# Hybrid decoder layer on one Trainium2 core: keys and values of the memory branch as one product of a transposed, unnormalised mem

## The chip, the cores and the metric

One core of a Trainium2 chip runs the whole layer as one program. The metric is the device time of an execution in microseconds (us). TensorE (PE in the views, its weight loads PEld) multiplies; VectorE (DVE), ScalarE (ACT) and GpSimd (POOL) do the rest; the queue of SyncE (SP) issues nearly all DMAs.

## The reference, cut to what matters

`d` = 1024, `s` = 512 rows of `x`, `m` = 256 rows of `mem`, four cross heads of 64.

```python
h = rms_norm(x, g_mix)                       # x * rsqrt(mean(x*x, row) + eps) * g
proj = h @ w_in                              # q, k, v, index q/k/w, conv, qc, gates
...
mem_kv = (rms_norm(mem, g_mem) @ w_mem_kv).reshape(b, m, 2, N_CROSS_HEADS, HEAD_DIM)
y_mem = memory_attention(qc, mem_kv[:, :, 0], mem_kv[:, :, 1]) @ w_mem_out
...
x = x + merged @ w_o                         # then norm, gated conv MLP, final norm
```

## The kernel before

Every product is made of three in fp32r: each operand is split into a high part `hi` (a copy on ACT to fp32r) and a low part `lo` (on DVE, source minus `hi`), and `mm3` (L144 to L147) adds hi·hi, hi·lo and lo·hi in one PSUM bank. Weights go through `load` (a DMA on SP's queue into tile `raw`) and `split` (L154 to L156) into `whi`/`wlo`; each of these three tags has three buffers, so a fourth load waits until an earlier one is split.

The program's order is a list of priorities. A planner that simulates the engines puts the instructions of each engine in a fixed order, in which they then run; the DMAs marked `first` stay in program order on SP's queue.

The first stage works off the memory tokens. `norm_rows` squares a block of 128 rows on ACT with a running sum, makes the inverse root on POOL, and multiplies rows, root and gain in one DVE instruction into `xn`. `turn_rows` transposes `xn` in eight 128x128 pieces on PE (L173) into two PSUM banks, and splits these into `mT` (for mem) or `h` (for x). The gain `g_mem` is loaded as `gm`, broadcast to 128 partitions (512 KB). Then 48 matmuls of 256 columns give the values (tokens in rows, `mT` is the stationary operand), split into `VM`; 48 more give the keys already transposed (`w_k` is stationary), copied to `kf`, and with `halves` and `twice` to `KM`. Both are read only in the cross attention, far later.

The second stage makes value and index columns of `w_in` (`w_n`, four tiles of 256 rows and 424 columns) for four blocks of `x`: 24 matmuls of 424 columns for each block. In the source the norm of block b+1 stands behind the products of block b. Its index columns are rotated (`rn`) and transposed (L306, L309). From there on `project` multiplies further columns of `w_in` with all of `h`, 24 matmuls of 512 columns each.

Of the kernel before, what the change touches and what calls it, by code (L numbers as in the profile page):

```python
# [10 lines left out]
F32 = mybir.dt.float32  # L11
F32R = mybir.dt.float32r
# [78 lines left out]


@with_exitstack
def layer(ctx, tc, x, mem, g_mix, g_mem, g_ffn, g_final, w_in, w_n, w_k, w_v, w_cm, w_att, w_o, w_up, w_down,
          params, rope, rope_n, out):
    nc = tc.nc

# [8 lines left out]
    def bank(tag="mm"):  # L106
        return ps.tile([P, 512], F32, tag=tag, name="ps_" + tag, bufs=banks[tag])
# [13 lines left out]

    def load(src, sp=wp, bufs=3):
        raw = sp.tile(list(src.shape), F32, tag="raw", name="raw", bufs=bufs)
        return raw, nc.sync.dma_start(raw, src)

    def split_load(raw, sp=wp, bufs=3):
        shape = list(raw.shape)
        hi = sp.tile(shape, F32R, tag="whi", name="whi", bufs=bufs)
        lo = sp.tile(shape, F32R, tag="wlo", name="wlo", bufs=bufs)
        split(hi, lo, raw)  # L130
        return hi, lo

    def wsplit(src, sp=wp):
        raw, _ = load(src)
        with tc.high_priority(offset=400):
            return split_load(raw, sp)

# [6 lines left out]
    def mm3(o, sh, sl, mh, ml, first, last):  # L144
        nc.tensor.matmul(o, sh, mh, start=first, stop=False)  # L145
        nc.tensor.matmul(o, sh, ml, start=False, stop=False)  # L146
        nc.tensor.matmul(o, sl, mh, start=False, stop=last)  # L147

    def gemm(o, w, act, kc=KD, k0=0):
        for k in range(kc):  # L150
            mm3(o, w[0][:, k0 + k, :], w[1][:, k0 + k, :], act[0][:, k, :], act[1][:, k, :],
                k == 0, k == kc - 1)

    def split(hi, lo, src):  # L154
        nc.scalar.activation(hi, src, AF.Copy)  # L155
        nc.vector.tensor_sub(lo, src, hi.bitcast(F32))  # L156

    def norm_rows(src, g, tmp):

        xn = tmp.tile([P, D], F32, tag="xn", name="xn", bufs=2)  # L160
        st = tmp.tile([P, 2], F32, tag="st", name="st", bufs=2)
        nc.scalar.activation(xn, src, AF.Square, accum_out=st[:, 0:1])
        nc.gpsimd.tensor_scalar(st[:, 0:1], st[:, 0:1], 1.0 / D, EPS, op0=ALU.mult, op1=ALU.add)
        nc.gpsimd.tensor_tensor(out=st[:, 1:2], in0=st[:, 0:1], in1=mhalf, op=ALU.pow)
        nc.vector.scalar_tensor_tensor(xn, src, st[:, 1:2], g, op0=ALU.mult, op1=ALU.mult)
# [23 lines left out]
    def bcast(g, n):  # L189
        return bass.AP(tensor=g.tensor, offset=g.offset, ap=[[0, P], [1, n]])  # L190
# [7 lines left out]
    oat = (op.tile([P, 3, S], F32R, name="oath"), op.tile([P, 3, S], F32R, name="oatl"))  # L198
    ocv = (op.tile([P, 3, S], F32R, name="ocvh"), op.tile([P, 3, S], F32R, name="ocvl"))
    ome = (op.tile([P, 2, S], F32R, name="omeh"), op.tile([P, 2, S], F32R, name="omel"))  # L200
# [3 lines left out]
    g0 = g0p.tile([P, KD, S], F32, name="g0")  # L204


    cs = ExitStack()
# [12 lines left out]

    es = ExitStack()
    ea = es.enter_context(pool("ea", side="right"))
    gm = ea.tile([P, D], F32, name="gm")
    gx = ea.tile([P, D], F32, name="gx")
    ropeN = ea.tile([P, 2, NB, 4], F32, name="ropeN")
    nc.scalar.dma_start(ropeN, rope_n)


    def first(dma):
        tc.keep_in_program_order(dma)  # L230

    def first_rows(src, b, slot):
        t = ea.tile([P, D], F32, tag=f"in{slot}", name="rows")
        first(nc.sync.dma_start(t, src[b * P:(b + 1) * P, :]))
        return t

    def first_load(src, *where):
        raw, dma = load(src, *where)
        first(dma)
        return raw  # L240
# [8 lines left out]
    mT = (ea.tile([P, KD, M], F32R, name="mTh"), ea.tile([P, KD, M], F32R, name="mTl"))  # L249
    norm_T(memn[0], gm, mT, 0, ea)  # L250
    wv[0] = split_load(wv[0])
    norm_T(memn[1], gm, mT, 1, ea)
    wk.append(first_load(w_k[1]))
    wn3 = first_load(w_n[3], ea, 1)
    wv[1] = split_load(wv[1])
    wn = [first_load(w_n[0])]
    xin.append(first_rows(x, 1, 0))
    wk[0] = split_load(wk[0])
    wn.append(first_load(w_n[1]))
    for b in range(MB):  # L260
        bs = slice(b * P, (b + 1) * P)
        pv = bank()
        for k in range(KD):
            w = wv[k // 4]
            mm3(pv[:, :CW], mT[0][:, k, bs], mT[1][:, k, bs], w[0][:, k % 4], w[1][:, k % 4], k == 0, k == KD - 1)
        split(VM[:, b, :, 0:HD], VM[:, b, :, HD:], pv[:, :CW].rearrange("p (h d) -> p h d", d=HD))
    norm_T(xin[0], gx, h, 0, ea)
    wk[1] = split_load(wk[1])
    wn.append(first_load(w_n[2]))
    xin += [first_rows(x, 2, 1), first_rows(x, 3, 2)]  # L270
    wn = [split_load(wn3, ea, 1)] + [split_load(w) for w in wn]
    kf = []
    for t in range(2):
        pb = bank()
        gemm(pb[:, :M], wk[t], mT)
        kf.append(ea.tile([P, M], F32, tag="kf", name="kf", bufs=2))
        nc.scalar.activation(kf[t], pb[:, :M], AF.Copy)
# [35 lines left out]

    def twice(K, r, j, hd, lo):
        a, q = slice(64 * j, 64 * j + 64), slice(64 - 64 * j, 128 - 64 * j)
# [495 lines left out]
```

## Time and profile before

| | us |
|---|---|
| runs | 1946.31, 762.21, 762.58 |
| median | 762.58 |
| profiled execution, its own time | 763.54 |
| its span, first to last instruction | 761.8 |
| TensorE busy in the span | 743.9 (98%) |
| VectorE busy | 465.9 (61%) |
| ScalarE busy | 339.1 (45%) |

The span lacks what lies around the first and the last instruction, 1.74 us of the profiled execution's time. Busy time is summed over the whole span and says nothing about a single stage.

### The profile page before, as it was taken

Reading aid. Unit: us, or ns where it says so; the run is one execution under the profiler, and the core shown is the slowest. Engines: PE = TensorE matmul, PEld = TensorE weight load, DVE = VectorE, ACT = ScalarE, POOL = GpSimd, SP = SyncE. Lnnn points to the kernel's source line nnn. Section 1 sums busy time; section 2 is a strip of 40 time slices with the busy share of each in tenths; the row PEclk is TensorE's granted clock in tenths of the full one; section 3 lists DMA queues with packets and bytes.
Section 4 is the critical chain, followed back from the end, with each engine's and each line's share of the span. In section 5 each row is a group of like instructions: output and inputs, shape, how many; then the busy total and the mean of one; then the engine's idle time right before and its main releaser. Section 6 shows DMA issues by size and latency. Waiting matters only on the chain.

```text
span 761.8 us, 9285 instructions
## 1 busy us (share of the span) xinstructions
PE 743.9 (98%) x3518; PEld 624.3 (82%) x3518; DVE 465.9 (61%) x793; ACT 339.1 (45%) x562; POOL 21.2 (3%) x49
## 2 busy tenths in 40 slices
PE   5999999999999999999999999999999999999996
PEld 4988888888888888888889888888888888888884
DVE  5744999999677765366465666566656664222225
ACT  5748545667455653234335343434343433121214
POOL 2100002000000000000010000000000000000001
PEclk9999999999999999999999999999999999999998
DMA  8623423532222223443502323232323232323202
GB/s 315 223 89 100 141 84 111 165 97 73 73 90 61 68 74 107 155 140 112 184 28 84 105 89 104 91 105 88 106 88 108 87 105 66 125 92 98 96 28 111
DMA packets 25181, 81.28 MB, mean 107 GB/s; under 512 B 3280, under 2 KB 4432, under 8 KB 25136
## 3 DMA queue, kind: packets, MB, share of 16 engines
q1 hardware_dynamic: 24848, 80.41, 32.0%
q8 instruction: 27, 0.44, 0.2%
q10 hardware_dynamic: 288, 0.28, 0.1%
q14 instruction: 18, 0.15, 0.1%
HBM read 75.24 MB, written 2.10 MB: 102 GB/s over the span
## 4 chain that ended last, share of the span: by engine, by line
PE 95%; DVE 2%; DMA 1%; ACT 1%; issue 1%; SPq 0%; POOL 0%; POOLq 0%; DVEq 0%
PE ps_mm L147 19%; PE ps_mm L145 19%; PE ps_mm L146 19%; PE ps_at L145 9%; PE ps_at L146 9%; PE ps_at L147 9%; PE ps_at L569 1%; PE ps_o L600 1%; PE ps_at L586 1%; PE ps_o L145 1%; PE ps_o L147 1%; PE ps_o L146 1%; PE ps_at L173 1%; DMA gm<-g_mem 1%; PE ps_at L380 1%
## 5 line engine op out<-in xcount | busy, mean ns | idle before, releaser
L156 DVE TENSOR_TENSOR wlo<-raw,whi 128x1024 fp32r<-128x1024 f32 (+3 forms) x133 | 157.2, 1185 | 198.3 <-ACT whi L155 198.3
L155 ACT ACTIVATE whi<-raw 128x1024 fp32r<-128x1024 f32 (+3 forms) x133 | 136.8, 1030 | 195.1 <-PE ps_o L147 82.1
L145 PE MATMUL ps_mm<-hhi,whi 128*128 128x512 f32 x312 | 122.5, 393 | 0.0
L146 PE MATMUL ps_mm<-hlo,whi 128*128 128x512 f32 x312 | 122.2, 392 | 0.0
L147 PE MATMUL ps_mm<-hhi,wlo 128*128 128x512 f32 x312 | 122.1, 392 | 0.0
L146 PE MATMUL ps_at<-h2l,whi 128*128 128x512 f32 (+1 forms) x216 | 78.9, 366 | 0.0
L147 PE MATMUL ps_at<-h2h,wlo 128*128 128x512 f32 (+1 forms) x216 | 78.9, 365 | 0.0
L145 PE MATMUL ps_at<-h2h,whi 128*128 128x512 f32 (+1 forms) x216 | 78.7, 366 | 0.0
L146 PEld LDWEIGHTS ps_mm<-hlo,whi 128*128 128x128 f32 x312 | 58.7, 188 | 11.8
L147 PEld LDWEIGHTS ps_mm<-hhi,wlo 128*128 128x128 f32 x312 | 58.6, 188 | 11.6
L145 PEld LDWEIGHTS ps_mm<-hhi,whi 128*128 128x128 f32 x312 | 58.6, 188 | 11.6
L145 PE MATMUL ps_mm<-h2h,whi 128*128 128x512 f32 x160 | 62.2, 389 | 0.0
L146 PE MATMUL ps_mm<-h2l,whi 128*128 128x512 f32 x160 | 62.2, 389 | 0.0
L147 PE MATMUL ps_mm<-h2h,wlo 128*128 128x512 f32 x160 | 62.2, 389 | 0.0
L147 PEld LDWEIGHTS ps_at<-h2h,wlo 128*128 128x128 f32 x216 | 40.7, 189 | 6.6
L146 PEld LDWEIGHTS ps_at<-h2l,whi 128*128 128x128 f32 x216 | 40.8, 189 | 6.4
L145 PEld LDWEIGHTS ps_at<-h2h,whi 128*128 128x128 f32 x216 | 40.6, 189 | 6.6
L145 PEld LDWEIGHTS ps_mm<-h2h,whi 128*128 128x128 f32 x160 | 30.0, 188 | 6.3
L147 PEld LDWEIGHTS ps_mm<-h2h,wlo 128*128 128x128 f32 x160 | 30.0, 188 | 6.3
L146 PEld LDWEIGHTS ps_mm<-h2l,whi 128*128 128x128 f32 x160 | 30.0, 188 | 6.1
L733 ACT ACTIVATE t<-t 128x512 f32<-128x512 f32 x22 | 13.9, 632 | 44.6 <-DVE t L415 44.5
L155 ACT ACTIVATE acth<-t 128x512 fp32r<-128x512 f32 x14 | 8.8, 632 | 40.4 <-DVE t L734 40.4
(246 smaller groups left out, 1316.0 us busy)
## 6 DMA issues: line engine op xcount, KB each, us to landing
raw<-w_up SPq DMA_DIRECT2D x44, 512.0 KB, 3.4
raw<-w_in SPq DMA_DIRECT2D x39, 512.0 KB, 3.3
raw<-w_down SPq DMA_DIRECT2D x22, 512.0 KB, 3.4
raw<-w_o SPq DMA_DIRECT2D x8, 512.0 KB, 3.5
raw<-w_cm SPq DMA_DIRECT2D x8, 320.0 KB, 2.9
rows<-x SPq DMA_DIRECT2D x4, 512.0 KB, 7.0
x<-x SPq DMA_DIRECT2D x4, 512.0 KB, 5.9
raw<-w_n SPq DMA_DIRECT2D x4, 424.0 KB, 5.8
```

The costliest lines, as they stand in the source:

```text
L145: nc.tensor.matmul(o, sh, mh, start=first, stop=False)
L146: nc.tensor.matmul(o, sh, ml, start=False, stop=False)
L147: nc.tensor.matmul(o, sl, mh, start=False, stop=last)
L155: nc.scalar.activation(hi, src, AF.Copy)
L156: nc.vector.tensor_sub(lo, src, hi.bitcast(F32))
L173: nc.tensor.transpose(pt[:, k * P:(k + 1) * P], xn[:, (4 * h + k) * P:(4 * h + k + 1) * P], ident)
L380: nc.tensor.matmul(pb[:, :W], Q4[:, hd, (b - 1) * P:b * P], K4[:, :W], start=True, stop=True)
L569: nc.tensor.matmul(pb[:, :N], QS[:, hd, b * P:(b + 1) * P], KS[i][:, g, :N], start=(i == 0), stop=(i == 1))
L586: nc.tensor.transpose(pt[:, kb * P:(kb + 1) * P], lt[:, kb * P:(kb + 1) * P], ident)
L600: nc.tensor.matmul(po[:, q0:], V[:, kb, g, :], PT[i][:, c], start=(kb == 0 and i == 0), stop=(kb == NB - 1 and i == 1))
L733: nc.scalar.activation(tt[0], tt[0], AF.Silu)
```

## The change

- `mem` is also passed to the program transposed (`memt`, features in partitions), and `g_mem` as a 128x8 array, so that the gain is one number for each partition and 128-feature slice. `mh` and `ml` (high and low part of gain times transposed mem) are made from the loaded tile directly, in eight slices of 128x256; no PE transposes and no row norm stand ahead of them.
- `w_k` and `w_v` become `w_kv`, four tiles of 256 rows and 512 columns (the first in two halves). Keys and values of 128 tokens are one product of 512 columns, over 8 slices, three matmuls, two blocks: 48 matmuls.
- The inverse root of each token's row is applied to the product (`memory_out`): scaled copies to `kr` and `VM`. The rows of `mem` are still loaded, later, for the square sum alone. The keys are transposed by four PE transposes and copied to `kf`.
- Loads, splits and norms are put in another order: memt and `w_kv` in turns first, then x, `w_n`, and mem's rows; the norm of x's block b+2 stands behind the products of block b. `w_n`'s parts have tiles of their own, and `first` keeps the order of all these DMAs.
- Early tiles share memory with the tiles of later attention outputs and gates (`oat`, `ocv`, `ome`, `g0`), which are therefore allocated later.

```diff
+    def inv_rms(src, st, dump):
+        nc.scalar.activation(dump, src, AF.Square, accum_out=st[:, 0:1])
+        nc.gpsimd.tensor_scalar(st[:, 0:1], st[:, 0:1], 1.0 / D, EPS, op0=ALU.mult, op1=ALU.add)
+        nc.gpsimd.tensor_tensor(out=st[:, 1:2], in0=st[:, 0:1], in1=mhalf, op=ALU.pow)
+        return st[:, 1:2]
...
+    gm = ea.tile([P, KD], F32, name="gm")
...
+    nc.scalar.dma_start(gm, g_mem)
     nc.scalar.dma_start(ropeN, rope_n)
...
-    memn = [first_rows(mem, 0, 0)]
-    first(nc.sync.dma_start(gm, bcast(g_mem, D)))
-    memn.append(first_rows(mem, 1, 1))
-    wv = [first_load(w_v[i]) for i in range(2)]
-    wk = [first_load(w_k[0])]
-    xin = [first_rows(x, 0, 2)]
+    mraw = [op.tile([P, KD // 2, M], F32, tag=t, name="mraw") for t in ("omeh", "omel")]
+    mT = g0p.tile([P, 2, KD, M], F32R, tag="g0", name="mT")
+    mh, ml = mT[:, 0], mT[:, 1]
+    wkv = []
+    for c in range(KD // 2):
+        parts = 2 if c == 0 else 1
+        raw = wp.tile([P, 2, 2 * CW], F32, tag="raw", name="raw", bufs=3)
+        for i in range(0, 2, 2 // parts):
+            k, n = 2 * c + i, 2 // parts
+            first(nc.sync.dma_start(mraw[k // 4][:, k % 4:k % 4 + n], memt[:, k:k + n]))
+            first(nc.sync.dma_start(raw[:, i:i + n], w_kv[c][:, i:i + n]))
...
+        if c == 2:
+            xin = [first_rows(x, 0, op, "ocvh")]
     first(nc.sync.dma_start(gx, bcast(g_mix, D)))
...
+    xin.append(first_rows(x, 1, op, "ocvl"))
+    for i in range(4):
+        raw = wp.tile([P, 2, NW], F32, tag="raw", name="raw", bufs=3)
+        first(nc.sync.dma_start(raw, w_n[i]))
...
+    memn = [first_rows(mem, 0, op, "oath")]
+    xin.append(first_rows(x, 2, ea, "in2"))
+    memn.append(first_rows(mem, 1, op, "oatl"))
+    xin.append(first_rows(x, 3, ea, "in3"))
+    pkv = [bank("o"), bank()]
+    for c, (raw, hi, lo, n) in enumerate(wkv):
+        for i in range(0, 2, n):
+            for k in range(2 * c + i, 2 * c + i + n):
+                src = mraw[k // 4][:, k % 4]
+                nc.scalar.activation(mh[:, k], src, AF.Copy, scale=gm[:, k:k + 1])
+                nc.vector.scalar_tensor_tensor(ml[:, k], src, gm[:, k:k + 1], mh[:, k].bitcast(F32), op0=ALU.mult,
+                                               op1=ALU.subtract)
+            split(hi[:, i:i + n], lo[:, i:i + n], raw[:, i:i + n])
+            for k in range(2 * c + i, 2 * c + i + n):
+                for b in range(MB):
+                    bs = slice(b * P, (b + 1) * P)
+                    mm3(pkv[b], mh[:, k, bs], ml[:, k, bs], hi[:, k % 2], lo[:, k % 2], k == 0, k == KD - 1)
+        if c == 2:
+            norm_T(xin[0], gx, h, 0, ea)
+    for raw, hi, lo in wn[:2]:
+        split(hi, lo, raw)
+    norm_T(xin[1], gx, h, 1, ea)
+    for raw, hi, lo in wn[2:]:
+        split(hi, lo, raw)
+    def memory_out(b, kr):
+        st = ea.tile([P, 2], F32, tag="st", name="st", bufs=2)
+        r = inv_rms(memn[b], st, memn[b])
+        v = pkv[b][:, CW:].rearrange("p (h d) -> p h d", d=HD)
+        nc.scalar.activation(kr, pkv[b][:, :CW], AF.Copy, scale=r)
+        nc.scalar.activation(VM[:, b, :, 0:HD], v, AF.Copy, scale=r)
+        nc.vector.scalar_tensor_tensor(VM[:, b, :, HD:], v, r, VM[:, b, :, 0:HD].bitcast(F32), op0=ALU.mult,
+                                       op1=ALU.subtract)
...
     for b in range(NB):
...
-        if b + 1 < NB:
-            norm_T(xin[b + 1], gx, h, b + 1, ea)
+        if b + 2 < NB:
+            norm_T(xin[b + 2], gx, h, b + 2, ea)
...
+        if b < MB:
+            memory_out(b, krow[b])
+    pk = bank("at")
+    for t in range(2):
+        for b in range(MB):
+            c = t * M + b * P
+            nc.tensor.transpose(pk[:, c:c + P], krow[b][:, t * P:(t + 1) * P], ident)
+    kf = ea.tile([P, 2, M], F32, name="kf")
+    nc.scalar.activation(kf, pk.rearrange("p (t m) -> p t m", t=2), AF.Copy)
```

## Rows read from the trace of the kernel before

**Rows 1.** The profile's page: the span, and busy time of each engine.

```profile
span 761.8 us, 9285 instructions
...
PE 743.9 (98%) x3518; PEld 624.3 (82%) x3518; DVE 465.9 (61%) x793; ACT 339.1 (45%) x562; POOL 21.2 (3%) x49
```

**Rows 2.** Busy time by stretch: PE, PEld, DVE, ACT, POOL; granted clock, DMA share, GB/s.

```profile
0.00:26.80 26.80, 17.84 (x120) 17.06 (x121) 16.59 (x20) 17.45 (x29) 4.58 (x17) 1.00 0.83 300
100.00:400.00 300.00, 300.00 (x1446) 251.09 (x1445) 220.02 (x448) 146.44 (x272) 11.71 (x24) 1.00 0.32 101
740.00:762.00 22.00, 14.40 (x64) 11.61 (x62) 11.26 (x25) 8.02 (x20) 3.40 (x4) 0.89 0.24 96
```

**Rows 3.** Timeline of the first stage: start, duration, what ran, idle time and releaser.

```profile
0.72 0.40 ACTq L226 DMA_DIRECT2D ropeN<-rope_n  x1
...
4.06 1.06 ACT L162 ACTIVATE xn<-rows 128x1024 f32<-128x1024 f32 x1 [1.62 <-DMA rows<-mem]
...
6.85 1.28 DVE L165 SCALAR_TENSOR_TENSOR xn<-rows,st,gm 128x1024 f32<-128x1024 f32 x1 [6.85 <-DMA gm<-g_mem]
...
8.18 1.97 PE L173 MATMUL ps_at<-ident,xn 128*128 128x128 f32 x8 [8.18 <-DVE xn L165]
...
13.16 0.58 PE L146 MATMUL ps_mm<-wlo,mTh 128*128 128x256 f32 x1
...
16.32 0.41 PE L145 MATMUL ps_mm<-mTh,whi 128*128 128x256 f32 x1
...
16.53 0.32 PE L146 MATMUL ps_mm<-wlo,mTh 128*128 128x256 f32 x1
...
16.69 0.28 PE L147 MATMUL ps_mm<-whi,mTl 128*128 128x256 f32 x1
...
16.81 0.28 PE L145 MATMUL ps_mm<-whi,mTh 128*128 128x256 f32 x1
...
20.95 1.04 PE L173 MATMUL ps_at<-ident,xn 128*128 128x128 f32 x8
...
26.85 0.35 PE L145 MATMUL ps_mm<-whi,hhi 128*128 128x424 f32 x1
```

**Rows 4.** Timeline of TensorE in the second stage.

```profile
30.03 0.35 PE L145 MATMUL ps_mm<-whi,hhi 128*128 128x424 f32 x1
30.22 0.35 PE L146 MATMUL ps_mm<-wlo,hhi 128*128 128x424 f32 x1
...
32.84 0.46 PE L146 MATMUL ps_mm<-wlo,hhi 128*128 128x424 f32 x1 [0.91 <-DVE wlo L156]
...
39.53 0.46 PE L145 MATMUL ps_mm<-whi,hhi 128*128 128x424 f32 x1 [0.25 <-ACT hhi L155]
...
51.14 0.35 PE L147 MATMUL ps_mm<-whi,hlo 128*128 128x424 f32 x1
```

**Rows 5.** DMA issues: queue, count, KB, us from issue to landing.

```profile
ropeN<-rope_n ACTq DMA_DIRECT2D x1, 16.0 KB, 3.5
```

**Rows 6.** Groups of instructions by shape, 0 to 52 us: count, busy us, mean ns.

```profile
L156 DVE TENSOR_TENSOR wlo<-raw,whi 128x1024 fp32r<-128x1024 f32 x7 | 8.3, 1222 | 1.0 <-ACT whi L155 1.0
...
L156 DVE TENSOR_TENSOR hlo<-ps_at,hhi 128x512 fp32r<-128x512 f32 x8 | 5.4, 686 | 1.8 <-ACT hhi L155 1.8
...
L165 DVE SCALAR_TENSOR_TENSOR xn<-rows,st,gx 128x1024 f32<-128x1024 f32 x4 | 5.1, 1279 | 2.9 <-POOL st L164 2.9
...
L155 ACT ACTIVATE hhi<-ps_at 128x512 fp32r<-128x512 f32 x8 | 4.5, 594 | 0.1
...
L156 DVE TENSOR_TENSOR wlo<-raw,whi 128x848 fp32r<-128x848 f32 x4 | 4.2, 1038 | 0.7 <-ACT whi L155 0.7
...
L156 DVE TENSOR_TENSOR hvl<-kf,hvh 128x256 fp32r<-128x256 f32 x2 | 0.8, 416 | 0.0
...
L277 ACT ACTIVATE kf<-ps_mm 128x256 f32<-128x256 f32 x2 | 0.7, 372 | 0.0
```

**Rows 7.** The chain of work that ended last, one piece of 512 columns.

```profile
52.28 0.23 PE ps_mm L145
```

More of the change, by code (lines that the diff above doesn't have):

```diff
@@ L93, in layer @@
 @with_exitstack
-def layer(ctx, tc, x, mem, g_mix, g_mem, g_ffn, g_final, w_in, w_n, w_k, w_v, w_cm, w_att, w_o, w_up, w_down,
+def layer(ctx, tc, x, mem, memt, g_mix, g_mem, g_ffn, g_final, w_in, w_n, w_kv, w_cm, w_att, w_o, w_up, w_down,
           params, rope, rope_n, out):
@@ L123, in load @@
         raw = sp.tile(list(src.shape), F32, tag="raw", name="raw", bufs=bufs)
-        return raw, nc.sync.dma_start(raw, src)
+        nc.sync.dma_start(raw, src)
+        return raw
     def split_load(raw, sp=wp, bufs=3):
@@ L133, in wsplit @@
     def wsplit(src, sp=wp):
-        raw, _ = load(src)
+        raw = load(src)
         with tc.high_priority(offset=400):
@@ L161, in norm_rows @@
         st = tmp.tile([P, 2], F32, tag="st", name="st", bufs=2)
[L162 to L165, printed above, removed]
+        r = inv_rms(src, st, xn)
+        nc.vector.scalar_tensor_tensor(xn, src, r, g, op0=ALU.mult, op1=ALU.mult)
         return xn
@@ L197, in layer, with op_pair @@
     op = os_.enter_context(pool("op"))
-    oat = (op.tile([P, 3, S], F32R, name="oath"), op.tile([P, 3, S], F32R, name="oatl"))
-    ocv = (op.tile([P, 3, S], F32R, name="ocvh"), op.tile([P, 3, S], F32R, name="ocvl"))
-    ome = (op.tile([P, 2, S], F32R, name="omeh"), op.tile([P, 2, S], F32R, name="omel"))
+    def op_pair(name, k):
+        return tuple(op.tile([P, k, S], F32R, tag=name + i, name=name + i) for i in "hl")
     sc = [op.tile([P, P * (b + 1)], F32, name=f"sc{b}") for b in range(1, NB)]
@@ L203, in layer @@
     g0p = os_.enter_context(pool("g0p"))
-    g0 = g0p.tile([P, KD, S], F32, name="g0")
     cs = ExitStack()
@@ L222, in layer @@
     ea = es.enter_context(pool("ea", side="right"))
-    gm = ea.tile([P, D], F32, name="gm")
+    gm = ea.tile([P, KD], F32, name="gm")
     gx = ea.tile([P, D], F32, name="gx")
     ropeN = ea.tile([P, 2, NB, 4], F32, name="ropeN")
+    nc.scalar.dma_start(gm, g_mem)
     nc.scalar.dma_start(ropeN, rope_n)
@@ L230, in first, with first_rows @@
         tc.keep_in_program_order(dma)
-    def first_rows(src, b, slot):
-        t = ea.tile([P, D], F32, tag=f"in{slot}", name="rows")
+    def first_rows(src, b, p, tag):
+        t = p.tile([P, D], F32, tag=tag, name="rows")
         first(nc.sync.dma_start(t, src[b * P:(b + 1) * P, :]))
         return t
[L237 to L240, printed above, removed]
-    memn = [first_rows(mem, 0, 0)]
-    first(nc.sync.dma_start(gm, bcast(g_mem, D)))
@@ L244, in layer @@
-    memn.append(first_rows(mem, 1, 1))
-    wv = [first_load(w_v[i]) for i in range(2)]
-    wk = [first_load(w_k[0])]
-    xin = [first_rows(x, 0, 2)]
-    first(nc.sync.dma_start(gx, bcast(g_mix, D)))
[L249 to L277, printed above, removed]
+    mraw = [op.tile([P, KD // 2, M], F32, tag=t, name="mraw") for t in ("omeh", "omel")]
+    mT = g0p.tile([P, 2, KD, M], F32R, tag="g0", name="mT")
@@ new lines, in layer @@
+    mh, ml = mT[:, 0], mT[:, 1]
[7 more added lines that the diff above has]
+            first(nc.sync.dma_start(raw[:, i:i + n], w_kv[c][:, i:i + n]))
+        hi = wp.tile([P, 2, 2 * CW], F32R, tag="whi", name="whi", bufs=3)
+        lo = wp.tile([P, 2, 2 * CW], F32R, tag="wlo", name="wlo", bufs=3)
+        wkv.append((raw, hi, lo, 2 // parts))
+        if c == 2:
+            xin = [first_rows(x, 0, op, "ocvh")]
@@ new lines, in layer @@
+    first(nc.sync.dma_start(gx, bcast(g_mix, D)))
+    xin.append(first_rows(x, 1, op, "ocvl"))
+    wn = []
+    for i in range(4):
+        raw = wp.tile([P, 2, NW], F32, tag="raw", name="raw", bufs=3)
+        first(nc.sync.dma_start(raw, w_n[i]))
+        wn.append((raw, ea.tile([P, 2, NW], F32R, name=f"wnh{i}"), ea.tile([P, 2, NW], F32R, name=f"wnl{i}")))
+    memn = [first_rows(mem, 0, op, "oath")]
+    xin.append(first_rows(x, 2, ea, "in2"))
+    memn.append(first_rows(mem, 1, op, "oatl"))
@@ L280, in layer @@
+    krow = [ea.tile([P, CW], F32, name=f"kr{b}") for b in range(MB)]
     for b in range(NB):
@@ L282, in layer @@
         pn = bank()
-        turn = (0, 1, 2, 3) if b == 0 else (1, 2, 3, 0)
-        for i in turn:
+        for i in range(4):
             for j in range(2):
-                k = 2 * ((3, 0, 1, 2)[i]) + j
-                mm3(pn[:, :NW], h[0][:, k, bs], h[1][:, k, bs], wn[i][0][:, j], wn[i][1][:, j],
-                    i == turn[0] and j == 0, i == turn[3] and j == 1)
-        if b + 1 < NB:
-            norm_T(xin[b + 1], gx, h, b + 1, ea)
+                k = 2 * i + j
+                mm3(pn[:, :NW], h[0][:, k, bs], h[1][:, k, bs], wn[i][1][:, j], wn[i][2][:, j], k == 0, k == KD - 1)
+        if b + 2 < NB:
+            norm_T(xin[b + 2], gx, h, b + 2, ea)
         split(V[:, b, :, 0:HD], V[:, b, :, HD:], pn[:, :KV].rearrange("p (g d) -> p g d", g=NG))
@@ L320, in layer @@
     for t in range(2):
-        lo = halves(kf[t], ea, M)[1]
+        lo = halves(kf[:, t, :], ea, M)[1]
         for j in range(2):
-            twice(KM, kf[t], j, 2 * t + j, lo)
+            twice(KM, kf[:, t, :], j, 2 * t + j, lo)
     nc.sync.dma_start(par, params)
@@ L326, in layer @@
     es.close()
+    oat, ocv, ome = op_pair("oat", 3), op_pair("ocv", 3), op_pair("ome", 2)
+    g0 = g0p.tile([P, KD, S], F32, tag="g0", name="g0")
     def project(c0):
@@ L790 @@
     add("mem", w["mem"])
-    for n in ("g_mix", "g_mem", "g_ffn", "g_final"):
+    add("memt", w["mem"].reshape(M, KD, P).transpose(2, 1, 0))
+    add("g_mix", w["g_mix"].reshape(1, D))
+    add("g_mem", w["g_mem"].reshape(KD, P).T)
+    for n in ("g_ffn", "g_final"):
         add(n, w[n].reshape(1, D))
@@ L795 @@
     add("w_n", np.stack([col_blocks(w["w_in"][i:i + 2 * P], [C_V], NW)[0] for i in range(0, D, 2 * P)]))
-    add("w_k", col_blocks(w["w_mem_kv"], range(0, CW, P)))
-    add("w_v", np.stack([col_blocks(w["w_mem_kv"][i:i + 512], [CW], CW)[0] for i in (0, 512)]))
+    add("w_kv", np.concatenate([col_blocks(w["w_mem_kv"][i:i + 2 * P], [0], 2 * CW) for i in range(0, D, 2 * P)]))
     add("w_cm", np.concatenate([col_blocks(w["w_conv_out"], wide), col_blocks(w["w_mem_out"], wide)], axis=2))
```

## The prediction

> **What bounds the kernel now.** The page comes first: TensorE is busy 743.9 of 761.8 us [rows 1]. The busy time by stretch says where the other 18 are: none between 100 and 400 us, 7.6 in the last 22 us, which the change doesn't touch, and 9.0 in the first 26.8 us, which it rewrites [rows 2]. So the kernel is bound by TensorE, and the change can win only TensorE's own instructions, its wait at the start, and its waits in the first 52 us. What DVE, ACT or a DMA saves counts only where TensorE waits for it.
>
> The timeline of the first stage shows that wait in three steps [rows 3]. ACT begins the first square at 4.06, when mem's rows are there. DVE can't apply the gain until 6.85: it waits for the broadcast `gm`, and the root had been ready by then. TensorE begins at 8.18, with transposes. Its first 256-column matmuls start 0.21 us apart (16.32, 16.53), then 0.12 apart (16.69, 16.81): that is 1.2 and then 2.4 GHz, though the clock column of this stretch reads 1.00 [rows 2]. So about half the stage's work ran at the low level. Eight transposes took 1.97 us early and 1.04 later. At 26.85 the products of the second stage begin.
>
> The second stage ends with the matmul at 51.14, that is at 51.33, so it takes 24.5 us [rows 3, 4]. Its own work is 4 x 24 matmuls 0.19 apart (18.2), 24 transposes of x's blocks 1 to 3 (3.1) and four of index rows (4 x 0.13, a share of the 1.04: 0.5). The rest, some 2.7 us, is lost: 0.91 to `wlo` at 32.84, and small waits for `hhi` and `hlo` as at 39.53, since a block's norm and transposes come just ahead of its products [rows 4].
>
> **The change part by part.** I follow TensorE to the end of the second stage, since later work is the same and TensorE is the bound there.
>
> Start. The first matmul needs memt's first slice (128 KB), `w_kv`'s first half (256 KB), the 4 KB of `gm`, one `mh` and one `hi`. The 512 KB of mem's rows had landed at 4.06, more than both transfers together [rows 3]. `gm` now goes ahead of `ropeN` on ACT's queue; `ropeN`, likewise a small piece for each partition, was issued at 0.72 and took 3.5 us, so I put `gm` at 4.2 [rows 3, 5]. An `mh` of 256 columns is bounded by the 0.37 of `kf`, a `hi` of 512 by the 0.59 of `hhi` [rows 6]: 4.2 + 0.4 + 0.6 = 5.2. Bounds: 4.6, if the `hi` is made while `gm` is under way; 7.3, if `gm` takes the 5.6 us that the broadcast needed (from 1.2 to 6.85 [rows 3]). I take 5.2, because `ropeN` is the nearer in size and queue. The Trainium skill ("DMA: Bandwidth & Descriptors", Specifications) speaks against this edit: transfers under 512 B don't run at line rate, and `gm` is 32 B for each partition. No row here has pieces that short; if the rule made `gm` as late as the broadcast, the start would be the 7.3 and the gain 2.1 us less.
>
> Memory products. Out go 96 matmuls of 256 columns and 16 transposes; in come 48 of 512. The columns are the same (24,576), at 0.23 us for 512 [rows 7] 11.0 us. The 16 transposes go altogether; the 8 of x's block 0 (1.04) stay in this stage. The low clock costs on top: a 512-column matmul then takes 2 x 0.21 = 0.42 us instead of 0.23, so each us at the low level loses 0.45. Before the rise at 16.6, TensorE had run matmuls without a pause for 3.4 us (from 13.16), and had worked at all for 8.4 (from 8.18) [rows 3]. The new stage has matmuls alone, as the 3.4 had, so I take 3.4 x 0.45 = 1.5; the other end is 3.8.
>
> I add one wait of 0.9 for a split, of the size of the one at 32.84, because the planner's order, made before the run, puts TensorE behind some `wlo` or `xn` here too. Bounds 0 and 1.8. End of the stage: 5.2 + 11.0 + 1.0 + 1.5 + 0.9 = 19.6, against 26.85.
>
> Second stage. TensorE needs the fourth `w_n` tile after 18 matmuls, at 19.6 + 3.4 = 23.0. On DVE must be done before: 8 `ml` (by `hvl`'s 0.42: 3.4), 4 `wlo` of 1024 (4.9), two blocks of x (each 1.28 and 2 x 0.69: 5.3) and 4 `wlo` of 848 (4.2), 17.8 us [rows 6]. From the first `ml` at 4.6 without a gap that ends at 22.4; at the share that DVE had between its start and 26.8 (16.59 of 19.95, 0.83 [rows 2]) at 26.0. So the wait is between 0 and 3.0, and I take 1.8, nearer to the row's share, because the first slices are spaced by their data. The DMAs come out alike: memt 1.05, `w_kv` 2.10, two blocks of x and `gx` 1.57, `w_n` 1.74, together 6.5 MB, at the 300 GB/s of this stretch [rows 2] 21.5 us, and two splits later 23.5.
>
> The stage's own work stays at 21.8, plus four transposes of `kr` (4 x 0.13, 0.5). Of the old 2.7 of waits nothing is left in my sum but the 1.8: the norm of block b+2 has the 4.6 us of block b+1's matmuls as cover, more than its square (1.06), its gain (1.28) and a first pair of splits (0.59 + 0.69) [rows 3, 6]. If that cover fails, the part of the 2.7 that isn't the 0.91 at `wlo` comes back, 1.8. So 24.1 us, and the end is at 43.7 instead of 51.3: 7.6 us less; I say 7.5.
>
> What I cost at nothing. `memory_out`'s squares, copies and `VM` splits are queued on ACT, POOL and DVE behind a block's rotation, and a square waits there for mem's rows, which now come after `w_n`: behind it on ACT stand the next block's `hhi` and the splits of `w_in`. By the order of the DMAs mem's second block lands behind 8.0 MB, at 27 us; the two squares stand behind products that end at about 26 and 31, so I see no wait; a late one would cost TensorE what the next `hhi` and `hlo` take, 1.3. mem is read twice (1.05 MB more) and the broadcast's 0.52 MB goes, a net 1.8 us of DMA at 300 GB/s, in front of loads that have time. `KM` and `VM` come some us later and are wanted far behind 100 us. The two product banks stay taken until `memory_out`; three `mm` banks for one product at a time are enough. The shared tiles (`ocv`, `g0`) are free long before their second use.
>
> **The sum.** 763.54 - 7.5 = 756.0 for an execution like the profiled one. That one lay 1.0 above the median of 762.58, so the median comes to 755.1, 1.0% less. A measurement of this kernel tells a change of about 2% from none, so this would count as the same.
>
> **The rivals.**
> - The start moves little: `gm` late (7.3), the clock up after 8.4 us (3.8), the 0.9 wait. The stage ends at 24.0, the fourth tile is then in time, and the second stage takes 22.3 with no wait or 25.0 with the old ones: gains of 5.0 or 2.3, 757.6 or 760.3. For it: the share of DVE and the DMA share of 0.83 [rows 2], so that everything early contends. Against it: no broadcast stands in front.
> - Everything fits: start 4.6, clock after 3.4 us, no wait in the first stage, 18.1; DVE without a gap lets the fourth tile come at 22.4, 0.9 after TensorE wants it. End 41.3, gain 10, 752.6. For it: DVE's work shrinks by two norms of 1.28 and gains 0.7 in smaller pieces. Against it: the 0.83.
> - Slower. The raw buffers turn into a chain: `w_n`'s last tile may only be issued after its first is split, that after a load behind `w_kv`'s second split, and all of SP's later loads (x's blocks 2 and 3, mem) stand behind it in fixed order. If the planner also lets x's norms go first on DVE, TensorE stands at the fourth tile. It decides from a landing at about 30 us on, 9 later than wanted; at 33 the median is 2.7 above before, 765.3, and more if the clock falls in the gap. Against it: even the sum of DVE at 0.83 ends at 26.
> - The change doesn't do what it says: the planner puts x's transposes or splits ahead and the memory products begin where they begin now, near 11 to 13; only the transposes and small waits are won, 0 to 2 us, 761.5.
>
> **How the numbers follow.** Forecast 0.6 (753.4 to 757.0), late start 0.2, everything fits 0.12, no effect 0.05, slower 0.03. The predicted time is that of the forecast, 755.1. The range reaches from the second rival's 752.6 to just under the first's 760.3. A gain of over 2% would need 15 us, twice the forecast: nearly all of TensorE's idle time and 16 transposes in the first 26.8 us and all the waits of the second stage (9.0 + 4 + 2.7), the first loads' own time included, so faster has 0.02; slower by 15 us would need a gap that no row hints at, 0.03 for the planner's order going wrong.
>
> **What would show it.** In the changed profile: TensorE's first instruction is a 512-column matmul at about 5; the step from 0.42 to 0.23 us apart comes before 10; the first 424-column matmul with `h` starts at about 19.6, the last ends at about 44; the wait in the second stage's first block names `wlo` or its DMA; the second half of the trace is the old one moved by 7.5. I am wrong if TensorE's first wait is for something else than `gm` or `w_kv`, if the clock rises as late as now, if the order on TensorE has a long gap between 5 and 20, or if the work behind 50 us changes in length.

## The result and the profile after

The changed kernel takes 776.65 us (median of four runs, 775.77 to 777.23). The kernel before, beside it, took 762.21, 762.58 and 764.18, and one slow execution of 1946.31 is left out. The ratio is 1.0179, with an interval of 1.0165 to 1.0193. The forecast was 755.1. The kernel got slower and not faster, and its time lies over 16 us above the range.

The profiled execution took 775.77, with a span of 774.0. Two lines of its page answer to [rows 1]:

```profile
span 774.0 us, 9178 instructions
...
PE 745.5 (96%) x3458; PEld 621.7 (80%) x3458; DVE 465.1 (60%) x796; ACT 341.6 (44%) x568; POOL 22.5 (3%) x49
```

TensorE stands still for 28.5 us instead of 17.9 and is busy 1.6 us longer, together the 12.2 us by which the span grew. The view that sums TensorE's waits by releaser shows where it waits (the columns: total us, times, longest us):

```profile
PE ps_at L419 <- DMA Q<-hvl: 10.2, 3, 9.2
PE ps_o L146 <- ACT whi L156: 5.5, 1, 5.5
PE ps_mm L146 <- ACT rn L320: 4.1, 1, 4.1
PE ps_o L147 <- DVE wlo L157: 0.5, 1, 0.5
```

The second line is the start. The first and the third are new, and the forecast has neither. The timeline of TensorE places them:

```profile
5.53 0.79 PE L146 MATMUL ps_o<-whi,mT 128*128 128x512 f32 x1 [5.53 <-ACT whi L156]
...
9.96 0.63 PE L147 MATMUL ps_mm<-wlo,mT 128*128 128x512 f32 x1
10.39 0.61 PE L148 MATMUL ps_mm<-whi,mT 128*128 128x512 f32 x1
...
12.92 0.40 PE L147 MATMUL ps_mm<-wlo,mT 128*128 128x512 f32 x1
13.16 0.40 PE L148 MATMUL ps_mm<-whi,mT 128*128 128x512 f32 x1
...
20.22 1.03 PE L178 MATMUL ps_at<-ident,xn 128*128 128x128 f32 x8
21.50 0.46 PE L146 MATMUL ps_mm<-wnh,hhi 128*128 128x424 f32 x1 [0.25 <-ACT hhi L156]
...
32.13 1.03 PE L178 MATMUL ps_at<-ident,xn 128*128 128x128 f32 x8
37.30 0.46 PE L146 MATMUL ps_mm<-wnh,hhi 128*128 128x424 f32 x1 [4.14 <-ACT rn L320]
...
77.11 0.55 PE L419 MATMUL ps_at<-K,Q 128*128 128x256 f32 x1 [9.20 <-DMA Q<-hvl]
```

The memory stage came out much as forecast: TensorE starts at 5.53, its matmuls of 512 columns are 0.43 apart at first and 0.24 apart from about 11 on, and the products of `x` begin at 21.50 where they began at 26.85 [rows 3], 5.35 us ahead. Blocks 0 and 1 are through at 32.13, where they were through at 38.14: 6.0 us ahead. Then come two gaps. I call the one ahead of 37.30 the **bank gap** (by what its wait names) and the one ahead of 77.11 the **index gap**. Busy time by stretch (PE, PEld, DVE, ACT, POOL; granted clock, DMA share, GB/s) shows that each gap is followed by low clock:

```profile
20.20:32.10 11.90, 11.57 (x65) 10.66 (x64) 8.52 (x10) 6.76 (x11) 2.31 (x4) 1.00 0.77 293
32.00:42.00 10.00, 5.48 (x23) 4.64 (x22) 7.86 (x21) 8.38 (x17) 2.71 (x5) 0.83 0.36 129
60.00:67.70 7.70, 7.70 (x39) 6.34 (x37) 1.75 (x3) 6.04 (x14) 0.00 (x0) 1.00 0.30 88
67.70:83.00 15.30, 5.15 (x13) 3.68 (x13) 7.03 (x12) 12.72 (x24) 0.00 (x0) 0.67 0.56 174
```

In this execution, behind the bank gap nine matmuls of 424 columns run 0.35 apart instead of 0.19, behind the index gap seven of 512 columns run 0.43 apart instead of 0.23. With the waits, the index gap costs 10.2 + 7 x 0.20 = 11.6 us, the bank gap 4.1 + 0.4 + 9 x 0.16 = 5.9. From about 150 us on, the work stands 12.0 to 12.3 us later than before (the first `ocvh` at 216.3 instead of 204.0), so all of it is lost ahead of that.

ACT's timeline shows what each gap is made of. In the bank gap:

```profile
28.17 1.06 ACT L160 ACTIVATE xn<-rows 128x1024 f32<-128x1024 f32 x1 [1.70 <-DMA rows<-x]
...
32.27 0.47 ACT L299 ACTIVATE kr<-ps_o,st 128x256 f32<-128x256 f32 x1 [1.91 <-POOL st L162]
...
33.16 1.06 ACT L160 ACTIVATE xn<-rows 128x1024 f32<-128x1024 f32 x1
...
34.35 1.07 ACT L156 ACTIVATE whi<-raw 128x1024 fp32r<-128x1024 f32 x1
35.30 1.07 ACT L160 ACTIVATE rows<-rows 128x1024 f32<-128x1024 f32 x1
...
36.34 0.61 ACT L156 ACTIVATE hhi<-ps_at 128x512 fp32r<-128x512 f32 x1
36.82 0.43 ACT L320 ACTIVATE rn<-ps_mm 128x288 f32<-128x288 f32 x1
```

TensorE's next product needs `hhi` of x's block 2, and a free bank, which the copy `rn` releases. Both stand at the end of a fixed order: behind the wait for x's rows, the wait for mem's root, two later squares and a split for `w_in`. They end 0.3 us apart (`hhi` at 36.95, `rn` at 37.25). In the index gap:

```profile
60.91 0.60 ACT L348 ACTIVATE kf<-ps_at 128x512 f32<-128x512 f32 x1
...
61.86 3.39 ACT L353 ACTIVATE km<-kf 64x256 fp32r<-64x256 f32 x8
65.28 1.06 ACT L156 ACTIVATE whi<-raw 128x1024 fp32r<-128x1024 f32 x1
...
67.72 1.06 ACT L156 ACTIVATE whi<-raw 128x1024 fp32r<-128x1024 f32 x1 [1.08 <-PE ps_mm L147]
68.68 0.61 ACT L400 ACTIVATE K<-rK 32x512 fp32r<-32x512 f32 x1
...
69.62 8.00 ACT L411 ACTIVATE Q<-rQ 32x384 fp32r<-32x384 f32 x15
```

The rotated index rows (`rK` and `rQ`) are ready at 61.0. In the kernel before they are ready at 60.0, and `K` and `Q` follow them at once; the first score needs no wait. ACT's timeline before, then TensorE's:

```profile
60.37 0.62 ACT L361 ACTIVATE K<-rK 32x512 fp32r<-32x512 f32 x1
...
61.30 8.04 ACT L372 ACTIVATE Q<-rQ 32x384 fp32r<-32x384 f32 x15
```
```profile
69.73 0.28 PE L380 MATMUL ps_at<-K,Q 128*128 128x256 f32 x1
```

In the changed kernel they come 8 us later, behind `kf`, KM's eight copies and two splits, while TensorE's order wants the first score at 67.75.

### The profile page after: what moved, and what is told of

It is laid out like the page before. It is cut to its first block, busy times and chain, and to the rows that moved or that the text cites. A ratio compares the mean times of both kernels' runs of the same rounds, so it can differ in the third digit from the quotient of the medians.

```text
span 774.0 us, 9178 instructions
## 1 busy us (share of the span) xinstructions
PE 745.5 (96%) x3458; PEld 621.7 (80%) x3458; DVE 465.1 (60%) x796; ACT 341.6 (44%) x568; POOL 22.5 (3%) x49
## 4 chain that ended last, share of the span: by engine, by line
PE 91%; DMA 3%; DVE 1%; SPq 1%; ACT 1%; issue 1%; POOL 1%; POOLq 0%; ACTq 0%
PE ps_mm L146 19%; PE ps_mm L148 19%; PE ps_mm L147 19%; PE ps_at L146 9%; PE ps_at L148 9%; PE ps_at L147 9%; DMA rows<-x 2%; PE ps_at L608 1%; PE ps_o L639 1%; PE ps_at L625 1%; PE ps_o L147 1%; PE ps_o L146 1%; PE ps_o L148 1%; DMA raw<-w_kv 1%; SPq L192 1%
## 5 line engine op out<-in xcount | busy, mean ns | idle before, releaser
L157 DVE TENSOR_TENSOR wlo<-raw,whi 128x1024 fp32r<-128x1024 f32 (+3 forms) x130 | 153.4, 1182 | 202.4 <-ACT whi L156 202.3
L156 ACT ACTIVATE whi<-raw 128x1024 fp32r<-128x1024 f32 (+3 forms) x130 | 133.4, 1028 | 194.6 <-PE ps_o L148 82.0
L146 PEld LDWEIGHTS ps_mm<-hhi,whi 128*128 128x128 f32 x312 | 59.0, 189 | 11.6
L434 DVE MAX8 m<-sc 128x8 f32<-128x256 f32 (+2 forms) x48 | 26.5, 555 | 0.6
```

The source lines that it names most:

```text
L434: nc.vector.max(m8, sc[b - 1])
```

## The experiments

Each kernel was timed against the kernel before on the same chip; the ratios compare them best. The diffs are against the changed kernel and cut to their core.

**The index gap: when the keys are made.** The transposes of `kr`, `kf` and KM's copies and moves become a function `keys()`. It is called right behind the second `memory_out`, or, with its tiles in a later pool and `kr` in the memory of mem's rows, ahead of the cross queries.

```diff
         if b < MB:
             memory_out(b, krow[b])
+        if b == MB - 1:
+            keys()
...
-    pk = bank("at")
...
-    kf = ea.tile([P, 2, M], F32, name="kf")
-    nc.scalar.activation(kf, pk.rearrange("p (t m) -> p t m", t=2), AF.Copy)
...
-        lo = halves(kf[:, t, :], ea, M)[1]
-        for j in range(2):
-            twice(KM, kf[:, t, :], j, 2 * t + j, lo)
```

> Undoes one move: the keys' transposes, kf and KM's copies and moves stand right behind the second memory_out instead of behind the fourth row block. Theory B (KM's work on ACT and on SP's queue, at 61 to 70 us, delays the index queries' copies and moves, for which TensorE waits 9.2 us at 77.1): the wait and the low clock behind it go, 11.5 us less than the changed kernel, about 765, with the first gap (33 to 37 us) unchanged. Rival (TensorE's planned order leaves nothing but the score matmuls there, whatever KM does): the wait stays within 2 us, 775 to 777.

> The same work moved the other way: behind the index scores, ahead of the cross queries. Theory B: the wait at 77 us goes as in the run before, about 765, if the late KM finds idle time on ACT before the cross attention; a wait of up to 3 us may come up at about 140 us. Rival (it is the age of KM, not its place): as before the edit, 775 to 777.

Early: 762.39, ratio 1.0001 (0.9991 to 1.0011). Late: 763.70, 1.0010 (1.0001 to 1.0020). Both ways the index gap is gone. Of the early one, the waits of TensorE that are left, in the same view as above:

```profile
PE ps_o L146 <- ACT whi L156: 5.7, 2, 5.5
PE ps_mm L146 <- ACT rn L340: 4.5, 1, 4.5
```

So the place of KM's work costs 13 to 14 us, and the bank gap stands by itself. What about that place costs is not told by this pair.

**The index gap: whose time?** One kernel issues KM's moves on GpSimd's queue instead of SP's, another makes KM's high-part copies on DVE instead of ACT.

```diff
-            move(K[1][c, hd, :], lo[a])
+            nc.gpsimd.dma_start(K[1][c, hd, :].bitcast(F32), lo[a].bitcast(F32))
```
```diff
-            nc.scalar.activation(K[0][c, hd, :], r[a], AF.Copy)
+            nc.vector.tensor_copy(K[0][c, hd, :], r[a])
```

> The changed kernel with only the eight moves of KM's low parts issued on GpSimd's queue in place of SP's; ACT's work for KM stays in front of the index queries. Theory (the index queries are late because ACT makes them behind KM's copies, and their moves are issued when they are ready): no change, 774 to 777, the wait for Q stays at 8 to 9 us. Rival (SP's 4.8 us of issuing KM's moves hold back the moves of K and Q and the loads of w_in): 4 to 5 less, 771 to 772, and Q's first move is issued before 70 where it was at 74.

> The changed kernel with KM's eight high-part copies (3.39 us on ACT) made on DVE instead; SP's moves stay. Theory (ACT's order is what makes Q late): ACT reaches the first Q copy 3 to 4 us earlier, the wait for Q falls from 9.2 to 5 or 6, and the time to 771 to 773. Rival (SP's queue is the limit): no change, 775 to 777. If the split copy of w_in on ACT, which waits for TensorE just ahead of K, is the limit: under 1 us.

Moves off SP: 778.28, ratio 1.0212 (1.0195 to 1.0229). Copies off ACT: 777.20, 1.0198 (1.0183 to 1.0214). Neither helps. So KM's moves on SP's queue aren't what costs, and my theory that KM's copies fill ACT (771 to 773) falls too. ACT's timeline of the second kernel shows it:

```profile
64.56 0.42 ACT L156 ACTIVATE hvh<-kf 128x256 fp32r<-128x256 f32 x1 [0.79 <-DVE hvl L157]
68.15 1.06 ACT L156 ACTIVATE whi<-raw 128x1024 fp32r<-128x1024 f32 x1 [3.17 <-PE ps_mm L147]
69.12 0.61 ACT L400 ACTIVATE K<-rK 32x512 fp32r<-32x512 f32 x1
```

ACT now has 3.17 us with nothing to do, the rows of `K` are long there, and still the copy to `K` comes behind the split `whi`, which waits for TensorE to release a buffer. It is the order that holds it: the planner put `K` there, as if it couldn't be written any earlier.

**The index gap: memory.** `kf` and its halves lie in the pool `ea` of the first stage, which is closed right behind them; the tiles of the index queries are allocated after that. One kernel gives all three tiles memory of the later attention outputs (tags `oath`, `ocvh`, `ocvl`, `omeh`, `omel`, all idle at this time) and changes neither an instruction nor the program's order. The other moves `kf` alone.

```diff
-    kf = ea.tile([P, 2, M], F32, name="kf")
+    kf = op.tile([P, 2, M], F32, tag="oath", name="kf")
-        lo = halves(kf[:, t, :], ea, M)[1]
+        lo = op.tile([P, M], F32R, tag=("ocvh", "ocvl")[t], name="hvl")
+        hi = op.tile([P, M], F32R, tag=("omeh", "omel")[t], name="hvh")
+        split(hi, lo, kf[:, t, :])
```

> The changed kernel with the keys where the change puts them; only kf and its halves get memory of the later attention outputs instead of the first stage's pool, which is closed right behind them. Theory now (the index queries' tiles reuse the memory of that pool, so they can't be written before kf and its halves have been read; that alone puts K and Q behind KM's copies and two w_in splits on ACT): K's copy stands on ACT right behind the last rotated rows, the wait for Q near 68 us goes, 762 to 764. Rival (KM's copies and moves take ACT's and SP's time in this stretch wherever they stand): the same instructions are all still there, ahead of the scores, so a wait for Q of 4 us or more stays, 768 or later. If neither is the cause: 775 to 777.

> As the run with kf and its halves in other memory, but only kf is moved; the halves stay in the first stage's pool. Theory (any tile of the closed pool that is read late holds the index queries): no gain, 774 to 777, the wait for Q stays at 8 to 10 us. Rival (kf, the largest of the three, is the tile that holds them): 762 to 766.

All three: 764.79, ratio 1.0020 (1.0011 to 1.0030). `kf` alone: 776.82, 1.0181 (1.0161 to 1.0201), with a wait for `Q` of 9.5. In ACT's timeline of the first, `K` now stands right behind `kf`, `Q` begins at 63.26, and KM's copies come after its first eight:

```profile
61.35 0.60 ACT L348 ACTIVATE kf<-ps_at 128x512 f32<-128x512 f32 x1
61.85 0.62 ACT L402 ACTIVATE K<-rK 32x512 fp32r<-32x512 f32 x1
...
67.89 0.83 ACT L353 ACTIVATE km<-kf 64x256 fp32r<-64x256 f32 x2
```

TensorE has no wait for `Q` any more; one of 1.12 for `rr` at 81.00 is left. So the same instructions on the same engines cost 12 us more or less by where three tiles of 1 or 2 KB a partition lie. The early keys tell the rest: there the same three tiles stay in the pool, are only read sooner, and the gap is gone as well. So it takes both, tiles of the closed pool and a late reader. Which tile of the index queries lies over which of the three was not traced.

**The bank gap.** Two edits, each alone, each with early keys, and both: the second memory product takes a bank of the other tag, so that three `mm` banks stay for the products of x; and x's blocks 2 and 3 are loaded behind the second `w_n` tile instead of behind the fourth.

```diff
-    pkv = [bank("o"), bank()]
+    pkv = [bank("o"), bank("at")]
```
```diff
     for i in range(4):
...
+        if i == 1:
+            xin += [first_rows(x, 2, ea, "in2"), first_rows(x, 3, ea, "in3")]
     memn = [first_rows(mem, 0, op, "oath")]
-    xin.append(first_rows(x, 2, ea, "in2"))
     memn.append(first_rows(mem, 1, op, "oatl"))
-    xin.append(first_rows(x, 3, ea, "in3"))
```

> The second memory product takes one of the four banks of the transposes instead of one of the three product banks. Bank theory (the third row block has no bank until the first is evacuated, so TensorE stands from 33.2 to 37.3 us): 4.5 us of wait and some 2 us of low clock go, about 770. Queue theory (ACT's fixed order has the squares of rows that land late ahead of the evacuation and of block 2's hhi): no change over 1 us, 775.5 to 777.5.

> Only the order of loads: rows of x's blocks 2 and 3 are loaded behind the second w_n tile, not behind the fourth, which waits on SP's queue for a raw buffer until 22.1 us. Queue theory: block 2's rows land near 19 instead of 28.1, its square and split come in time, the gap at 33 to 37 us shrinks by 4 us or more and with it the low clock, about 770. Bank theory: the gap stays, since the bank is still held, 775 to 777.

> Keys right behind the second block's copies, and the second memory bank taken from the other tag; x's blocks 2 and 3 loaded as in the change. Theory (two waits that end nearly together hold TensorE at 32 to 37 us, the bank's release and block 2's high parts, and each edit takes away one): the bank edit alone gives about 0.8, as it did without the key edit, so 761.6, and a wait of over 3 us near 36 stays, now for hhi. Rival (the two edits simply add, so that each carries its share of the 4.6 whatever the other does): 762.4 less 2 to 2.5, near 760. If the bank is the whole of it: 757.8.

> Keys right behind the second block's copies, and x's blocks 2 and 3 loaded behind the second w_n tile; the banks as in the change. Theory (two waits that end nearly together): about 2.2 less than with the keys alone, 760.2, and a wait of 1 to 3 us for rn stays near 37. Rival (the edits add): 762.4 less 2 to 2.5, which is the same number, so the sum of this run's gain and that of the bank's tells them apart: 3.0 with two parallel waits, 4.6 if they add. If the order of the loads is the whole of it: 757.8, and no wait for rn over 0.5.

> Three edits at once: the keys early, x's blocks 2 and 3 loaded behind the second w_n tile, and the second memory product in a bank of the transposes. Queue theory for the first gap: x's rows are in time, the bank is free, only memory_out's squares and copies and w_in's splits are left ahead of the evacuations on ACT: wait of 2 us or less at the third row block, 757 to 760. If the gap is made by mem's squares alone it stays near 4 us: 761 to 763.

| | us | ratio | wait in this place |
|---|---|---|---|
| the change | 776.65 | 1.0179 (1.0165 to 1.0193) | 4.14, `rn` |
| bank | 775.85 | 1.0167 (1.0147 to 1.0187) | 3.74, `hhi` |
| loads | 774.47 | 1.0155 (1.0136 to 1.0173) | 2.79, `rn` |
| early keys | 762.39 | 1.0001 (0.9991 to 1.0011) | 4.54, `rn` |
| early keys, bank | 762.82 | 1.0004 (0.9994 to 1.0014) | 3.92, `hhi` |
| early keys, loads | 760.60 | 0.9974 (0.9964 to 0.9984) | 2.79, `rn` |
| early keys, both | 757.83 | 0.9933 (0.9918 to 0.9948) | none over 1.4 |

The bank alone gains nothing, the loads alone 0.3%, both 0.7%. The releaser changes with the edit, here in the timelines of TensorE, first with early keys and bank, then with early keys and loads:

```profile
37.17 0.46 PE L146 MATMUL ps_mm<-wnh,hhi 128*128 128x424 f32 x1 [3.92 <-ACT hhi L156]
```
```profile
38.04 0.46 PE L146 MATMUL ps_mm<-wnh,hhi 128*128 128x424 f32 x1 [2.79 <-ACT rn L340]
```

That is two waits in parallel: take one away, and the other is there. The view had named only the later one. With early keys the two alone add up to 0.2%, which speaks against each having a share of its own. The theories of a single cause (near 770 for the bank or for the loads) fell with it, and of the 0.8 us that I expected from the bank behind early keys nothing came. With both edits the largest wait behind the start is the 1.38 here, the granted clock stays at 1.00 from 20 us on, and the kernel takes 0.7% less than the one before:

```profile
39.65 0.27 PE L351 MATMUL ps_at<-ident,rn 128*32 128x128 f32 x1 [1.38 <-DVE rn L348]
```

The waits of the table don't add up to the times, since what follows a wait differs. In the profiled executions 9 matmuls of 424 columns ran at the low clock behind the gap in the changed kernel, some 16 with early keys and some 16 with the loads alone, but none with early keys and loads, behind the same 2.79 as with the loads alone (in that execution the products of x began at 23.47, some two us later than in the other kernels).

Joined to the tiles in other memory, with the keys left where the change puts them, the two edits should give nearly the same:

> The changed kernel with kf and its halves in other memory, the second memory bank taken from the other tag, and x's blocks 2 and 3 loaded behind the second w_n tile; the keys stay where the change puts them. Theory (memory reuse is the whole of the wait for Q, and bank and loads the whole of the wait at 32 to 37 us): 757 to 760, as with the keys made early. Rival (KM's work in front of the scores costs by itself): 762 or later.

They gave 759.16, ratio 0.9948 (0.9934 to 0.9963), 1.3 us more than with early keys.

**Does the row norm on the product cost?** Three kernels with x loaded first. The first and the second have the early keys and the banks of the change. The first has no row norm of `mem`; the second makes the square sums from the transposed mem, where DVE squares the slices and TensorE sums them with a column of ones. The third has the late keys, the other bank, and both `memory_out` calls behind the loop over x's blocks. Their cores in turn:

```diff
-        r = inv_rms(memn[b], st, memn[b])
+        r = mone
```
```diff
+            nc.vector.tensor_mul(sq[k // 4][:, k % 4], src, src)
...
+            nc.tensor.matmul(pr[:, b:b + 1], sq[k // 4][:, k % 4, b * P:(b + 1) * P], mone, start=k == 0, stop=k == KD - 1)
...
-        r = inv_rms(memn[b], st, memn[b])
+        r = ri[:, 1, b:b + 1]
```
```diff
-        if b < MB:
-            memory_out(b, krow[b])
...
+    for b in range(MB):
+        memory_out(b, krow[b])
```

> Leaves out the row norm of mem: its rows are not loaded, not squared, and the products are copied out unscaled; keys early and x's rows early as before. What the late norm costs is the difference to the kernel with these two edits. If mem's rows and squares on ACT make the first gap: it closes, 755 to 757, where my forecast for the whole change was. If w_in's splits ahead of the evacuations make it: a wait of 2 to 3 us stays, 758 to 761.

> The whole computation with the row sums taken from memt: squares of its slices on DVE, summed over features by 16 small matmuls with a column of ones, so that the root is there when the product is, and mem's rows are not loaded at all; keys early, x's rows early. Queue theory: nothing on ACT waits for mem's rows; the 16 matmuls cost TensorE about 2 us, the first gap closes: 756 to 759, below both kernels. If the gap comes from w_in's splits: 760 to 763.

> memory_out is put behind the fourth row block in the program, the keys ahead of the cross queries, x's rows early, the product in a bank of the transposes. If memory_out's place in the program makes the first gap: it closes, 756 to 758. If the planner pulls the squares forward into ACT's idle time anyway, as its planned order shows, the gap depends on what stands ahead of the evacuations there: 758 to 762.

Without the norm: 757.75, 0.9930 (0.9915 to 0.9945). That is 2.9 less than with early keys and loads alone (760.60), and no more than the bank edit gives in the same place with the norm left in (757.83). So the norm seems to cost by the bank that it keeps taken; a kernel without the norm and with the other bank, which would show whether anything else is left, was not run. Sums from the transposed mem: 760.39, 0.9970 (0.9957 to 0.9983). TensorE then waits for nothing over 0.34 behind its start, but the sums, matmuls of a single column, take it 3.63 us at 20.79 where I expected some 2, and in the 8 us from 22 on, with TensorE busy throughout, the granted clock reads 0.86 and then 0.71. Calls behind the loop: 757.90, 0.9932 (0.9916 to 0.9949), the same as the combination.

**The start.** In the changed kernel the load of ACT's table stands behind the wait for memt (3.15 to 4.43 us); before it lay at 1.16, in front of the wait for mem's rows that ended at 4.06. ACT's timeline of the changed kernel:

```profile
3.15 1.28 ACT L279 ACT_TABLE_LOAD   x1 [3.15 <-DMA mraw<-memt]
...
4.86 0.61 ACT L156 ACTIVATE whi<-raw 128x512 fp32r<-128x512 f32 x1
```

One activation of a single column, from a constant, at the head of ACT's program moves it.

```diff
+    early = const.tile([P, 1], F32, name="early")
+    nc.scalar.activation(early, mhalf, AF.Copy)
```

> The kernel with early keys, loads of x first and the other bank (757.8, a ratio of 0.993), and one activation of a single column made from a constant at the head of ACT's program. Theory (the load of ACT's table, 1.28 us, stands in the changed kernel between memt's landing and the first mh, since it comes with the first activation and that one waits for memt; before it lay at 1.16 us, in front of the wait): TensorE starts 1.0 to 1.3 earlier, near 4.4, and the time falls by as much, to 756.5 to 757. Rival (the load is hidden, since the first half of w_kv lands no earlier): TensorE's start stays at 5.2 or later, 757.5 to 758.

757.77, 0.9936 (0.9923 to 0.9950): no gain. The rival was right, and ACT's timeline shows why:

```profile
1.64 1.28 ACT L234 ACT_TABLE_LOAD   x1 [1.64 <-PEq L824]
...
3.27 0.51 ACT L281 ACTIVATE mT<-mraw,gm 128x256 fp32r<-128x256 f32 x1
4.87 0.63 ACT L156 ACTIVATE whi<-raw 128x512 fp32r<-128x512 f32 x1 [1.08 <-DMA raw<-w_kv]
```

The first `mh` comes 1.2 us earlier, but `hi` waits for the first half of `w_kv`, which lands near 4.9 here. TensorE starts at 5.55. These are two waits in parallel once more: in the changed kernel the table load and `mh` fill the time up to 4.86, and without them the weights do.

## Why the prediction was wrong, point by point

- **What bounds the kernel** was right: TensorE, and only its waits early on could change. But I followed TensorE only "to the end of the second stage, since later work is the same". The later work is the same; its order isn't, and 11.6 us were lost from 67.75 on, behind the point where I stopped. One reading was off, though no term rests on it: of TensorE's 17.8 busy us in the first stage 7.6 lie ahead of the rise at 16.53, at half the rate, so about a quarter of the work ran at the low level and not half.
- **Start**: 5.2 forecast, 5.53 measured, near it by luck. `gm` landed 2.5 us after its issue, at 3.2 and not at 4.2, and the table load of 1.28, which my sum had at nothing, made up for it: 3.15 + 1.28 + 0.4 + 0.6 = 5.4. Without that load the weights of `w_kv` set the start, as the run above shows. The Trainium skill's rule on transfers under 512 B ("DMA: Bandwidth & Descriptors", Specifications), by which I had a start of 7.3, didn't decide here: `gm`'s 32 B for each partition took less than `ropeN`'s 128 B, which are under 512 B too, as the view of DMA issues has it (KB each, us from issue to landing):

```profile
gm<-g_mem ACTq DMA_DIRECT2D x1, 4.0 KB, 2.5
ropeN<-rope_n ACTq DMA_DIRECT2D x1, 16.0 KB, 3.8
```

- **Memory products**: TensorE is through with them and x's transposes at 21.5, not 19.6. The start has 0.3 of that; twelve matmuls ran at the low clock, which costs 2.4 (12 x 0.20) and not 1.5; the other 0.7 are pauses beyond the 0.9 in the sum. The mechanism was right, the term for the low clock 0.9 too small.
- **Second stage**: it ends at 53.4, not at 43.7; 1.9 of that is its later start, 5.9 the bank gap, and 2.8 are twelve 512-column products of `project` that now stand in between (12 x 0.23) and are no loss. The 1.8 for the fourth `w_n` tile did not come; its parts were ready in time. That makes 52.5; where the last 0.9 went was not traced. The cover that I gave to the norm of block b+2 failed: x's block 2 lands behind the fourth `w_n` tile and mem's first block, at 28.1, and its square waits for that.
- **The step that failed is "What I cost at nothing"**, in two of its sentences. "`KM` and `VM` come some us later and are wanted far behind 100 us" asked who reads KM, and not who waits for the memory that its sources hold. Its price is 12 to 14 us (the keys early or late, or the tiles elsewhere). The sentence on shared tiles had the right question, but asked it of `ocv` and `g0` alone. "Three `mm` banks for one product at a time are enough", with the squares that "I see no wait" for, is the other; with the load order it costs 5 us (1.0001 to 0.9933). I did name `memory_out`'s queue on ACT and what stands behind it, but at 1.3 us and for one late landing, without the low clock behind a pause.
- **The rivals**: the slower one was a chain through the raw buffers and x's loads behind the fourth `w_n` tile, at a chance of 0.03. Half of it is there (x's block 2 late by that chain, the clock falling in the gap), but its place was the fourth tile, and its size is the smaller gap's. The index gap had no rival at all.
- **With both gaps taken away** the forecast is nearly there: 757.83 against 755.1, a gain of 5.0 us of 7.5. Against the sum, the products of x begin 1.8 later (21.39), waits of 0.6 and 1.4 follow, and the 1.8 for the fourth tile is saved: 2.0 of the 2.5 that are missing.

## What to carry to other kernels

When a piece of work moves later, ask of each tile that it touches not only who reads the result but what memory its sources hold and who is allocated over them next; a closed pool can tie the next stage to the last reader of its slowest tile, as it did here. Two waits that end nearly together hide each other: an edit that gains nothing alone may be worth its full price behind another one, and a change of the releaser's name is the sign to look for. In a kernel bound by TensorE, a pause can cost more than its length: behind the two gaps here the low clock took 1.4 us each, and in other executions from nothing to some 2.6 (16 matmuls x 0.16).

## What the runs showed of the hardware

On POOL the small step of the root takes 0.19 us, but 1.16 while DVE multiplies a block of rows. POOL's timeline of the changed kernel, then DVE's:

```profile
29.41 0.19 POOL L161 TENSOR_SCALAR st<-st 128x1 f32<-128x1 f32 x1 [9.59 <-ACT xn L160]
...
30.45 1.16 POOL L161 TENSOR_SCALAR st<-st 128x1 f32<-128x1 f32 x1 [0.21 <-ACT rows L160]
```
```profile
30.27 1.29 DVE L170 SCALAR_TENSOR_TENSOR xn<-rows,st,gx 128x1024 f32<-128x1024 f32 x1 [2.72 <-POOL st L162]
```

The slow one ends at 31.61, just behind DVE's 31.56. The one at 36.55 took 1.18 beside a `wlo` of DVE from 36.46 to 37.68. Beside an instruction of DVE with one input in PSUM there is no delay: the root's second step at 37.81 took its usual 0.55 beside `hlo` (37.59 to 38.27). The Trainium skill says that a DVE instruction with two SBUF inputs and a GpSimd one that reads SBUF take a shared port in turns, each for its whole length ("SBUF — State Buffer", SBUF: two separate sides). These rows agree. The first of the two delays stands in the chain of the bank gap: the copy to `kr` waits 1.91 us for this root.

The load of ACT's table (1.28 us) is booked to the first activation, but whether it waits with it differs: it lay at 3.15 behind the wait for memt in the changed kernel, at 1.64 with the early activation, and in the kernel before at 1.16, 2.9 us ahead of the first activation (4.06), which waited for mem's rows. What decides this, no run here shows.
